# Feed-forward of a decoder trunk: five plain units for six, X put in the PSUM banks by ScalarE, half of the sums of seven products left to TensorE, one tile for the sums of a chunk pair

## The chip, the core and the metric

One core of a Trainium2 chip runs the whole program. The metric is the time of one execution on the device in microseconds (us); lower is better. In the profile PE is TensorE (PEld its weight loads), DVE is VectorE, ACT is ScalarE, POOL is GpSimd, SP is SyncE, which issues nearly all DMAs.

## The reference

A trunk of two layers on 512 tokens of width 1024, all in float32. Each layer is an attention part and a feed-forward part, and a final norm ends it. The attention part is not touched here. The feed-forward part, with 22 chunks of 128 channels in each half of `w_in` (D_FF = 2816):

```python
def conv_glu_ffn(h, w_in, conv_w, conv_b, w_out):
    a, b = jnp.split(h @ w_in, 2, axis=-1)                  # 1024 -> 2 x 2816
    a = causal depthwise convolution of width 3(a) + conv_b
    return (jax.nn.silu(a) * b) @ w_out                      # 2816 -> 1024

x = x + mixer(rmsnorm(x, attn_norm[layer]))
x = x + conv_glu_ffn(rmsnorm(x, ffn_norm[layer]), ...)       # layer 0, then layer 1
```

## The kernel before

**Layout.** Activations lie with channels on the partitions and the 512 tokens along the row. X is eight tiles of 128x512, `X[0]` to `X[7]`. A float32 operand is split in two parts, a rounded one (`h`, an ACT copy with cast) and the rest (`l`, a DVE subtraction), and each product is three matmuls: h by h, l by h, h by l. So every weight tile that is loaded (`wraw`, `wb`, `wo`) costs an ACT cast (`whi`, `sxh`) and a DVE subtraction (`wlo`, `sxl`) before its second matmul can start.

**A plain unit.** Chunk c of `a` or `b` is a unit: eight weight blocks times `XH[k]`, `XL[k]`, 24 matmuls 512 wide, into one PSUM bank (`mm`). Two units make a chunk. DVE multiplies the bank by `rstd` into `a` or `b`; `gate` does the convolution (ACT `tap2`, two DVE `tap`, ACT Silu), `gated` multiplies and splits the result into `gh`, `gl`. The first PLAIN = 6 chunks are done so.

**A seven.** The other 16 chunks are done by `seven(c)`: the 2x2 block product (weights of a and b, two halves of the 1024 channels, two halves of the tokens) with seven products of half the size in place of eight. Each product is 12 matmuls 256 wide. Weight sums `p1` to `p4` are made by `total` and split by `part`; products go to banks `s` (two buffers of two banks), `t` and `o`; seven DVE or ACT operations (`first_a`, `first_b`, `v`, `c12`, `both`, `c11`, `c21`) put the results together. The moving sides of the seven are sums of halves of the normed X, made once per layer by `sums(k)` for the four chunk pairs (k, k+4): two norms on DVE (`gh<-x,ng,rstd`), four 256-wide sums on POOL (`gl<-gh`), four splits. They are made beside the plain units.

**The output.** `out(m, p)` multiplies the gated chunks of part p (PARTS: chunks 0-5, 6-11, 12-16, 17-21) with a block of w_out into a bank `mm`, and DVE adds the bank to `X[m]`. In layer 1 the last part is done token-wise with the final norm (`tokens`).

**Who sets the order.** `Plan` is a list of jobs with engine, cost, dependencies, buffers taken and given, and a priority; `Plan.run` places them one by one and the instructions of every engine are emitted in that order. Engines run them in that order: an instruction that waits holds up all behind it on its engine.

The PE priorities are 100 + chunk for units and products and 200 + part for `out`, so that `out` fills the gaps that products leave:

```python
order[1] = add("PE", 1.45, fn, pj[n], order[1], *TJ, prio=100 + c, take=(take,), give=("slot",))
j = add("PE", 0.685, step, wj, j, GJ[c0 + k], prio=200 + p, ...)
```

All instructions are recorded at line 91 (a wrapper), so the profile's groups are told apart by tile names. `sr` names a weight sum, `sxh`/`sxl` its parts, `b1`, `b2`, `t1`, `t3` (h and l) the moving sums.

Of the kernel before, what the change touches and what calls it, by code (L numbers as in the profile page):

```python
# [18 lines left out]
P = 128  # L19
# [19 lines left out]
PARTS = ((0, 6), (6, 12), (12, 17), (17, 22))  # L39
PLAIN = 6  # L40
# [143 lines left out]
def trunk(ctx, tc, A):  # L184
# [10 lines left out]
    def mm(out, l, r, st, sp_):  # L195
        pe.matmul(out, l, r, start=st, stop=sp_)
# [943 lines left out]
    def ffn(layer, nl, final):  # L1140
# [7 lines left out]
        with ExitStack() as es:  # L1148
            fp = es.enter_context(tc.tile_pool(name=f"fp{layer}", bufs=2))
            first = [weights(A["wfi"][layer, u], [P, NK, P], behind=fed[0] if u else None) for u in range(2)]  # L1150
            plan = Plan(dict(PE=0.0, ACT=2.6, DVE=2.6, POOL=4.9, SP=-5.0), dict(PE=0.03), wraw=2, wb=2, wo=2, w=2, mm=2, s=2, t=1, o=1,
                        a=2, tt=1, b=2, g=10, sr=2, slot=NK, sq=2)
            plan.bufs["w"], plan.bufs["slot"] = [], []
            add = plan.add
            M = Mixer(plan, None, None)
            GH, GL, GJ = {}, {}, {}
            B = {n: [fp.tile([P, H, w], F32R, tag=f"{n}{x}", bufs=1, name=f"{n}{x}") for x in "hl"]
                 for n, w in (("b1", W), ("b2", SEQ), ("t1", SEQ), ("t3", SEQ))}

            MV = dict(b11=("b1", LO), b21=("b2", LO), b22=("b2", HI), t1=("t1", LO), t2=("t1", HI), t3=("t3", LO), t4=("t3", HI))  # L1160
# [4 lines left out]

            def split(h, l, x, n, prio, *deps, take=(), give=()):

                j = add("ACT", 0.19 + 0.00085 * n, lambda: act.copy(h(), x()), *deps, prio=prio, take=take)
                return add("DVE", 0.16 + 0.00104 * n, lambda: dve.tensor_sub(l(), x(), h().bitcast(F32)), j, prio=prio, give=give)
# [54 lines left out]
            def plain(c, root):  # L1224
                box = {}
                ps = []
                for u in range(2):
# [3 lines left out]
                    for k in range(NK):  # L1231
                        def step(k=k, w=w, bx=bx):
                            if k == 0:
                                bx["ps"] = mm_bank()
# [5 lines left out]
                        j = add("PE", 0.685, step, w[1], j, prio=100 + c, take=("mm",) if k == 0 else (), give=give)  # L1240
# [11 lines left out]
                j = add("DVE", 0.69, fa, ps[0][1], root[0], prio=1, take=("a",), give=("mm",))  # L1252
                t = gate(c, box, j)
                j = add("DVE", 0.69, fb, ps[1][1], prio=1, take=("b",), give=("mm",))
# [3 lines left out]
            def sums(k, root):  # L1258

                x = {}  # L1260

                def norm(c):
                    x[c] = g_tile("gh", F32)
                    dve.scalar_tensor_tensor(x[c], X[c], ng[:, nl - 1, c:c + 1], rstd, op0=ALU.mult, op1=ALU.mult)
                    if c >= H:
                        x["d1"], x["d3"] = g_tile("gl", F32), g_tile("gl", F32)
# [8 lines left out]
                part = lambda n, i: (lambda: B[n][i][:, k])  # L1275
                a = split(part("b1", 0), part("b1", 1), lambda: x[k][:, LO], W, p, j, s4)
                b = split(part("b2", 0), part("b2", 1), lambda: x[k + H], SEQ, p, j, s4, give=("g",))
                c = split(part("t1", 0), part("t1", 1), lambda: x["d1"], SEQ, p, s2, s4)
                d = split(part("t3", 0), part("t3", 1), lambda: x["d3"], SEQ, p, s4, c, b, give=("g",))
                TJ.extend((a, b, c, d))  # L1280

            order = [None] * 3
            count = [0]

            def seven(c):

                w, box, sm, sj = [None] * 4, {}, {}, {}
                n0 = c * 0.001

                def load(u, pool_, tag):  # L1290
                    def fn():
                        t = pool_.tile([P, NK, P], F32, tag=tag, bufs=2, name=tag)
# [3 lines left out]
                lb = add("SP", 0.35, load(1, fp, "wb"), M.prev_load, prio=1 + n0, take=("wb",), lat=3.3)  # L1296
                la = M.prev_load = add("SP", 0.35, load(0, wp, "wraw"), lb, prio=1 + n0, take=("wraw",), lat=3.3)

                def total(n, x, y, eng, *deps, give=()):
                    e = (pool, dve)[eng == "DVE"]  # L1300

                    def fn():
                        sm[n] = wp.tile([P, H, P], F32, tag="sq", bufs=2, name="sr")
                        e.tensor_add(sm[n], x(), y())
                    sj[n] = order[2] = add(eng, 1.35 if eng == "POOL" else 0.69, fn, *deps, order[2], prio=1.2 + n0, take=("sr",), give=give)
# [10 lines left out]
                E1, E3 = "DVE", "POOL"  # L1316
                total("p1", lambda: w[2], lambda: w[3], E1, lb)
                part("a1", lambda: w[0], la)
                total("p2", lambda: sm["p1"], lambda: w[0], "DVE", sj["p1"], la)
                part("p2", lambda: sm["p2"], sj["p2"])  # L1320
                part("p1", lambda: sm["p1"], sj["p2"], give=("sr",))
                total("p4", lambda: sm["p2"], lambda: w[1], "DVE", pj["p2"], pj["p1"], give=("sr",))
                part("p4", lambda: sm["p4"], sj["p4"], give=("sr",))
                total("p3", lambda: w[0], lambda: w[2], E3, sj["p4"])
                part("p3", lambda: sm["p3"], sj["p3"], give=("sr",))
# [3 lines left out]
                def product(j, n, m, take):  # L1329
                    t, cols = MV[m]  # L1330

                    def fn():
                        if take == "s":
                            r = box[j] = s_bank()[:, 0:W]
                        else:
                            r = box[j] = bank(names[take], take)[:, 0:W]
                        h, l = parts[n]
                        for k in range(H):
                            xh, xl = B[t][0][:, k, cols], B[t][1][:, k, cols]
                            mm(r, h[:, k], xh, k == 0, False)  # L1340
                            mm(r, l[:, k], xh, False, False)
                            mm(r, h[:, k], xl, False, k == H - 1)
                    order[1] = add("PE", 1.45, fn, pj[n], order[1], *TJ, prio=100 + c, take=(take,), give=("slot",))
# [14 lines left out]

                def both():
                    b = box["b"].rearrange("p (h s) -> p h s", h=2)  # L1360
# [463 lines left out]
```

## Time and profile before

| | |
|---|---|
| time, median of 3 runs (lowest, highest) | 1217.15 us (1217.04, 1217.43) |
| the profiled execution: time, its span | 1217.21 us, 1215.4 us |
| granted TensorE clock | 0.999 |
| busy share PE, DVE, ACT, POOL | 99%, 77%, 53%, 18% |
| layer 0: feed-forward starts; first seven starts | 271.4 us; about 338 us |
| layer 1: feed-forward starts; first seven starts | 855.4 us; about 921 us |
| POOL, all of it | 221.1 us in 262 instructions |

A matmul's row in the timeline lasts from its start to the end of its pipeline, so rows overlap: the pace of TensorE is the distance from one start to the next, and a wait shows as a longer distance. Time "idle before" an instruction is the engine's, with what released it. A row of several instructions ("x2") gives the time from the start of the first to the end of the last.

### The profile page before, as it was taken

The numbers are of one execution on the slowest core, as the hardware profiler recorded it, in microseconds if no ns is written. First come the engines' busy times: TensorE is split into PE (matmuls) and PEld (weight loads), VectorE is DVE, ScalarE is ACT, GpSimd is POOL, SyncE is SP. The second block draws the span as 40 slices with busy tenths as digits, with TensorE's granted clock in tenths as the row PEclk, the third lists the DMA queues.
The fourth block names the chain that finished last, engine by engine and source line by source line (L and its number), as shares of the span: only waits on it lengthen the run. The fifth ranks groups of instructions, "written<-read, shape, count | busy, mean of one in ns | idle before, by whom it ended". The sixth has DMA issues, their size and how long they took to land.

```text
span 1215.4 us, 19513 instructions
## 1 busy us (share of the span) xinstructions
PE 1204.9 (99%) x7476; PEld 1036.9 (85%) x7476; DVE 935.1 (77%) x1603; ACT 643.4 (53%) x1185; POOL 221.1 (18%) x262
## 2 busy tenths in 40 slices
PE   9999999999999999999999999999999999999997
PEld 6887877778898999999887888877888999999996
DVE  6867887579997999888764563456899889988885
ACT  6666577745553454444453664644555445444453
POOL 0000044423310011000121452411341001100000
PEclk9999999999999999999999999999999999999999
DMA  7322231122413231413224452322233233232331
GB/s 236 122 73 92 73 112 36 36 70 87 161 65 122 96 109 62 149 62 126 84 91 150 160 178 83 110 70 87 87 115 129 74 114 127 73 106 79 124 105 70
DMA packets 50685, 124.71 MB, mean 103 GB/s; under 512 B 6096, under 2 KB 16080, under 8 KB 50592
## 3 DMA queue, kind: packets, MB, share of 16 engines
q1 hardware_dynamic: 50304, 123.18, 30.6%
q8 instruction: 59, 0.97, 0.3%
q14 instruction: 34, 0.28, 0.1%
q10 hardware_dynamic: 288, 0.28, 0.1%
HBM read 119.80 MB, written 2.13 MB: 100 GB/s over the span
## 4 chain that ended last, share of the span: by engine, by line
PE 87%; DVE 8%; ACT 2%; issue 2%; POOL 1%; DMA 0%; SPq 0%; DVEq 0%; POOLq 0%; ACTq 0%
PE mm L91 50%; PE s L91 19%; PE t L91 11%; PE o L91 7%; DVE wlo L91 1%; DVE tt L91 1%; POOL e L91 1%; DVE b L91 1%; ACT e L91 1%; DVE sxl L91 1%; DVE gh L91 1%; DVE gl L91 0%; DMA wraw<-wu 0%; DVE a L91 0%; ACT ph L91 0%
## 5 line engine op out<-in xcount | busy, mean ns | idle before, releaser
L91 PE MATMUL mm<-xh,whi 128*128 128x512 f32 x424 | 168.7, 398 | 0.0
L91 PE MATMUL mm<-xh,wlo 128*128 128x512 f32 x424 | 165.5, 390 | 0.0
L91 PE MATMUL mm<-xl,whi 128*128 128x512 f32 x424 | 165.4, 390 | 0.0
L91 DVE TENSOR_TENSOR wlo<-wraw,whi 128x1024 fp32r<-128x1024 f32 (+2 forms) x83 | 100.8, 1214 | 45.0 <-ACT whi L91 44.8
L91 POOL TENSOR_TENSOR sr<-wraw,wb 128x512 f32<-128x512 f32 x32 | 47.4, 1482 | 462.9 <-DVE sr L91 288.1
L91 PE MATMUL mm<-gh,wlo 128*128 128x512 f32 x312 | 122.3, 392 | 0.0
L91 PE MATMUL mm<-gh,whi 128*128 128x512 f32 x312 | 122.2, 392 | 0.0
L91 PE MATMUL mm<-gl,whi 128*128 128x512 f32 x312 | 121.4, 389 | 0.0
L91 ACT CAST sxh<-sr 128x512 fp32r<-128x512 f32 x128 | 76.4, 618 | 83.9 <-DVE sr L91 54.9
L91 ACT CAST whi<-wraw 128x1024 fp32r<-128x1024 f32 (+2 forms) x83 | 81.8, 986 | 65.6 <-PE mm L91 41.8
L91 DVE TENSOR_TENSOR x<-x,mm 128x512 f32<-128x512 f32 x96 | 65.4, 684 | 47.8 <-PE mm L91 47.5
L91 POOL TENSOR_SCALAR e<-e,dn 128x128 f32<-128x128 f32 (+3 forms) x128 | 76.2, 616 | 135.6 <-DVE dn L91 123.2
L91 ACT ACTIVATE tt<-a,conv 128x512 f32<-128x512 f32 x44 | 35.9, 817 | 117.8 <-DVE a L91 117.8
L91 DVE TENSOR_TENSOR sxl<-sr,sxh 128x512 fp32r<-128x512 f32 x128 | 95.2, 761 | 2.7 <-ACT sxh L91 1.9
L91 PEld LDWEIGHTS mm<-xh,whi 128*128 128x128 f32 x424 | 79.6, 188 | 19.2 <-issue 3.7
L91 PEld LDWEIGHTS mm<-xl,whi 128*128 128x128 f32 x424 | 79.6, 188 | 17.2 <-DVE xl L91 0.5
L91 PEld LDWEIGHTS mm<-xh,wlo 128*128 128x128 f32 x424 | 79.7, 188 | 17.0 <-DVE wlo L91 1.6
L91 ACT ACTIVATE e<-e,nm 128x256 f32<-128x256 f32 (+3 forms) x128 | 70.7, 556 | 31.6 <-DVE nm L91 31.4
L91 DVE SCALAR_TENSOR_TENSOR tt<-a,conv,tt 128x510 f32<-128x510 f32 x88 | 72.5, 824 | 8.4 <-ACT tt L91 7.2
L91 PE MATMUL s<-t3l,sxh 128*128 128x256 f32 x256 | 72.4, 283 | 0.0
L91 PE MATMUL s<-t3h,sxl 128*128 128x256 f32 x256 | 72.4, 283 | 0.0
L91 PE MATMUL s<-t3h,sxh 128*128 128x256 f32 x256 | 72.4, 283 | 0.0
(281 smaller groups left out, 3420.8 us busy)
## 6 DMA issues: line engine op xcount, KB each, us to landing
wraw<-wfi SPq DMA_DIRECT2D x56, 512.0 KB
wb<-wfi SPq DMA_DIRECT2D x32, 512.0 KB
wraw<-wu SPq DMA_DIRECT2D x30, 512.0 KB
wo<-wfo SPq DMA_DIRECT2D x32, 384.0 KB
wraw<-wo SPq DMA_DIRECT2D x16, 512.0 KB
wo<-wfo SPq DMA_DIRECT2D x24, 320.0 KB
wraw<-wv SPq DMA_DIRECT2D x10, 512.0 KB
x<-x SPq DMA_DIRECT2D x16, 256.0 KB
```

The lines of the kernel that those rows point to most:

```text
L91: r = f(*a, **k)
```

## The change

1. PLAIN = 5, PARTS = (0-4, 5-10, 11-16, 17-21): one chunk more in each layer is done by `seven` (17 in place of 16). The first two `out` of part 0 are cut in two, so that chunk 4 comes last, and run ahead of the first seven.
2. PE order: units, sevens and outs have one counter (`turn`) as priority, 100 + place, so that a seven's products follow each other and one `out` follows each seven.
3. `out` of the parts 0 to 2 (but for m = 0, 1 of part 0): ACT copies `X[m]` into the bank ahead of the matmuls (`place`), these add onto it, and ACT copies the bank back to `X[m]`. The DVE addition goes.
4. In a seven, product 5 is added by TensorE onto product 0's bank and product 6 onto product 3's (`more`), ACT copies the first sum out (`c11`), `both` and the old `c11` go from DVE. The sum `p3` stays on POOL but needs the loaded weights alone (tile `sp`), and its product comes fourth, that of `p4` fifth. Banks 0 and 3 are the two halves of one tile `s`.
5. `sums(k)`: the two normed chunks and the six sums lie in one tile of 128x2048 (`SX`: `sx`, and for odd k the two `wb` buffers, so the first load into `wb` waits for the last `sums`). POOL makes the sums in three instructions (one 2x256 wide, two 256 wide) in place of four, ACT and DVE split all seven pieces in one instruction each of 128x1792 (`bh`, `bl`). Their priority is 1.2027 and the like (that of the weights of a plain unit is 1.2 + 0.001 per unit); it was 2.0 to 2.3.

```diff
-PARTS = ((0, 6), (6, 12), (12, 17), (17, 22))
-PLAIN = 6
+PARTS = ((0, 5), (5, 11), (11, 17), (17, 22))
+HOLD = 2
+PLAIN = 5
...
             def sums(k, root):
...
-                p = 2 + 0.1 * k
-                j = add("DVE", 0.75, lambda: norm(k), root[0], prio=p, take=("g",))
-                j = add("DVE", 0.75, lambda: norm(k + H), j, prio=p, take=("g",))
-                eng, e, cost = (pool, "POOL", 0.74) if True else (dve, "DVE", 0.42)
-                s1 = add(e, cost, lambda: eng.tensor_sub(x["d1"][:, LO], x[k][:, LO], x[k][:, HI]), j, prio=p)
-                s2 = add(e, cost, lambda: eng.tensor_add(x["d1"][:, HI], x[k + H][:, HI], x["d1"][:, LO]), s1, prio=p)
-                s3 = add(e, cost, lambda: eng.tensor_sub(x["d3"][:, LO], x[k + H][:, HI], x[k][:, HI]), s2, prio=p)
-                s4 = add(e, cost, lambda: eng.tensor_sub(x["d3"][:, HI], x["d1"][:, HI], x[k + H][:, LO]), s3, prio=p)
+                p = 1.2 + 0.0001 * (25,27,65,67)[k]
+                j = add("DVE", 0.75, lambda: norm(k), root[0], prio=p, take=("sx",) if n == 0 else ("wb", "wb"))
+                j = add("DVE", 0.75, lambda: norm(k + H), j, prio=p)
+                j = add("POOL", 1.48, lambda: pool.tensor_sub(two(4, 6), two(1, 3), hi.unsqueeze(1).to_broadcast([P, 2, W])), j, prio=p)
+                j = add("POOL", 1.1, lambda: pool.tensor_add(e1, hi2, d1), j, prio=p)
+                j = add("POOL", 1.1, lambda: pool.tensor_sub(e3, e1, lo2), j, prio=p)
+                j = add("ACT", 0.19 + 0.00085 * NC, lambda: act.copy(BX[0][:, k], x[:, W:]), j, prio=p)
+                TJ.append(add("DVE", 0.16 + 0.00104 * NC, lambda: dve.tensor_sub(BX[1][:, k], x[:, W:], BX[0][:, k].bitcast(F32)), j, prio=p,
+                              give=("sx",) if n == 0 else ("wb", "wb")))
...
-                lb = add("SP", 0.35, load(1, fp, "wb"), M.prev_load, prio=1 + n0, take=("wb",), lat=3.3)
+                lb = add("SP", 0.35, load(1, "wb"), M.prev_load, TJ[-1], prio=1 + n0, take=("wb",), lat=3.3)
...
-                j = product(4, "p3", "t3", "s")
-                c22 = take("DVE", 0.69, both, j, c12, give=("s",))
-                j = product(5, "a2", "b21", "t")
-                c11 = take("DVE", 0.42, lambda: dve.tensor_add(av(LO), av(LO), box[5]), j, u, give=("t",))
+                j = product(3, "p3", "t3", 1)
+                c22 = take("DVE", 0.42, lambda: dve.tensor_sub(bv(HI), av(HI), box[3]), j, v)
+                j = product(4, "p4", "b22", "t")
+                c12 = take("DVE", 0.42, lambda: dve.tensor_sub(av(HI), box[4], av(HI)), j, c22, give=("t",))
+                j = product(5, "a2", "b21", 0, kept, u, more=True)
+                c11 = take("ACT", 0.36, lambda: act.copy(av(LO), box[5]), j)
...
             def out(m, p, use=None, ready=None):
...
+                onto = (use is None or final) and (p > 0 or m > 1)
+                def place():
+                    bx["ps"] = M.bank("mm")
+                    if onto:
+                        act.copy(bx["ps"], X[m])
...
-                j = add("DVE", 0.69, lambda: dve.tensor_add(X[m], X[m], bx["ps"]), j, prio=1, give=("mm",))
+                    if onto:
+                        j = XO[m] = add("ACT", 0.62, lambda: act.copy(X[m], bx["ps"]), fo[0], prio=1, give=(bx["job"],))
```

Two places in the order of instructions. First DVE in the plain stage, from the second norm of the first chunk pair on (both layers alike). `gh<-x` and `wb<-x`, `sx<-x` are norms, `tt` the taps of the chunk before, `wlo<-wraw` the l weights of the fifth unit, without which its second matmul cannot start. Before:

```order
L91 SCALAR_TENSOR_TENSOR gh<-x_1652,ng,rstd 128x512
L91 TENSOR_TENSOR gl<-b,gh 128x512
L91 TENSOR_TENSOR a<-mm,rstd 128x512
L91 SCALAR_TENSOR_TENSOR gh<-x_1646,ng,rstd 128x512
L91 TENSOR_TENSOR wlo<-wraw,whi 128x1024
L91 SCALAR_TENSOR_TENSOR tt<-a,conv,tt 128x510
L91 SCALAR_TENSOR_TENSOR tt<-a,conv,tt 128x511
```

And now, where all lines are one further down:

```order
L92 SCALAR_TENSOR_TENSOR sx<-x_1652,ng,rstd 128x512
L92 TENSOR_TENSOR gl<-b,gh 128x512
L92 TENSOR_TENSOR a<-mm,rstd 128x512
L92 SCALAR_TENSOR_TENSOR wb<-x_1646,ng,rstd 128x2x256
L92 SCALAR_TENSOR_TENSOR wb<-x_1652,ng,rstd 128x512
L92 SCALAR_TENSOR_TENSOR tt<-a,conv,tt 128x510
L92 SCALAR_TENSOR_TENSOR tt<-a,conv,tt 128x511
L92 TENSOR_TENSOR wlo<-wraw,whi 128x1024
L92 TENSOR_TENSOR bl<-sx,bh 128x1792
```

The fifth unit's l weights have moved behind one norm more and both taps.

Second POOL in the feed-forward of layer 1, from the last instruction of the attention part on. Before, the sums of the four chunk pairs are sixteen short instructions, of which these are the first eight:

```order
L91 TENSOR_TENSOR acc<-acc,sq 128x512 x6
L91 TENSOR_TENSOR gl<-gh 128x256
L91 TENSOR_TENSOR gl<-gh,gl 128x256
L91 TENSOR_TENSOR gl<-gh 128x256
L91 TENSOR_TENSOR gl<-gl,gh 128x256
L91 TENSOR_TENSOR gl<-gh 128x256
L91 TENSOR_TENSOR gl<-gh,gl 128x256
L91 TENSOR_TENSOR gl<-gh 128x256
L91 TENSOR_TENSOR gl<-gl,gh 128x256
```

And now all of them, with the 17 weight sums of the sevens behind them:

```order
L92 TENSOR_TENSOR acc<-acc,sq 128x512 x6
L92 TENSOR_TENSOR sx<-sx 128x2x256
L92 TENSOR_TENSOR sx<-sx 128x256 x2
L92 TENSOR_TENSOR wb<-wb 128x2x256
L92 TENSOR_TENSOR wb<-wb 128x256 x2
L92 TENSOR_TENSOR sx<-sx 128x2x256
L92 TENSOR_TENSOR sx<-sx 128x256 x2
L92 TENSOR_TENSOR wb<-wb 128x2x256
L92 TENSOR_TENSOR wb<-wb 128x256 x2
L92 TENSOR_TENSOR sp<-wraw,wb 128x512 x17
```

The first sum of a pair no longer starts after its first norm but, with the others, after the second.

More of the change, by code (lines that the diff above doesn't have):

```diff
@@ L1279, in sums @@
-                d = split(part("t3", 0), part("t3", 1), lambda: x["d3"], SEQ, p, s4, c, b, give=("g",))
-                TJ.extend((a, b, c, d))
+                    out = x[:, SEQ:2 * SEQ] if c >= H else x[:, 0:SEQ].rearrange("p (h w) -> p h w", h=2)[:, ::-1]
+                    src, r = X[c], rstd
+                    if c < H:
+                        src, r = [t.rearrange("p (h w) -> p h w", h=2) for t in (X[c], rstd)]
+                    dve.scalar_tensor_tensor(out, src, ng[:, nl - 1, c:c + 1], r, op0=ALU.mult, op1=ALU.mult)
@@ L1290, in load @@
-                def load(u, pool_, tag):
+                turn[0] += 1
+                at = turn[0]
+                n0 = at * 0.001
+                def load(u, tag):
                     def fn():
-                        t = pool_.tile([P, NK, P], F32, tag=tag, bufs=2, name=tag)
+                        if u:
+                            wide[0] ^= 1
+                            t = WB[:, wide[0]]
+                        else:
+                            t = wp.tile([P, NK, P], F32, tag=tag, bufs=2, name=tag)
@@ L1343, in product @@
-                    order[1] = add("PE", 1.45, fn, pj[n], order[1], *TJ, prio=100 + c, take=(take,), give=("slot",))
+                            xh, xl = BX[0][:, k, cols], BX[1][:, k, cols]
+                            mm(r, h[:, k], xh, k == 0 and not more, False, more)
+                            mm(r, l[:, k], xh, False, False, more)
+                            mm(r, h[:, k], xl, False, k == H - 1, more)
+                    own = ("s",) if j == 0 else (place,) if place in names else ()
@@ L1344, in product @@
+                    order[1] = add("PE", 1.45, fn, pj[n], order[1], *TJ, *deps, prio=100 + at, take=own, give=("slot", *give))
                     return order[1]
@@ L1374, in seven @@
+                c12 = take("DVE", 0.42, lambda: dve.tensor_sub(av(HI), box[4], av(HI)), j, c22, give=("t",))
+                j = product(5, "a2", "b21", 0, kept, u, more=True)
+                c11 = take("ACT", 0.36, lambda: act.copy(av(LO), box[5]), j)
                 t = gate(c, box, c11, c12)
-                j = product(6, "b2", "t4", "s")
-                c21 = take("DVE", 0.42, lambda: dve.tensor_sub(bv(LO), bv(LO), box[6]), j, c22, give=("s",))
+                j = product(6, "b2", "t4", 1, c22, more=True)
@@ L1377, in seven, with out @@
+                c21 = take("DVE", 0.42, lambda: dve.tensor_sub(bv(LO), bv(LO), box[6]), j, give=("s",))
                 gated(c, box, t, c21)
-            fo = [None]
-            def out(m, p, use=None):
+            fo, pl, XO, gone = [None], [None], {}, [None, None]
+            def out(m, p, use=None, ready=None):
                 c0, c1 = PARTS[p]
@@ new lines, in end @@
+                def end():
+                    if onto:
+                        j = XO[m] = add("ACT", 0.62, lambda: act.copy(X[m], bx["ps"]), fo[0], prio=1, give=(bx["job"],))
+                    else:
+                        j = XO[m] = add("DVE", 0.69, lambda: dve.tensor_add(X[m], X[m], bx["ps"]), fo[0], XO.get(m), prio=1, give=(bx["job"],))
+                    gone.append(j)
+                    if use is not None:
+                        use(m, j)
+                steps(range(n - 1))
@@ L1476, in turn @@
                                     pe.transpose(bx["ps"][:, t, i * P:i * P + P], X[4 * h + i][:, (t0 + t) * P:(t0 + t) * P + P], ident)
[L1477 removed]
+                        j = add("PE", 0.9, turn, end, *(xj[m] for m in range(4 * h + 4)), prio=302.5 + 0.1 * h, take=("s",))
                         for t in (t0, t0 + 1):
```

175 lines of the change are left out of this document (88 added, 87 removed).

## The prediction

> **What bounds the kernel now.** I read the busy shares first, then the four stages of the two feed-forward parts by windows (columns: stretch, length, then busy time and count of PE, PEld, DVE, ACT, POOL, then clock, DMA share, GB/s), then two long stretches of the chain that ends last.
>
> ```profile
> PE 1204.9 (99%) x7476; PEld 1036.9 (85%) x7476; DVE 935.1 (77%) x1603; ACT 643.4 (53%) x1185; POOL 221.1 (18%) x262
> ...
> 272.00:337.60 65.60, 65.60 (x287) 53.31 (x286) 61.68 (x81) 37.26 (x55) 21.20 (x17) 1.00 0.34 120
> 337.60:595.00 257.40, 257.14 (x1762) 239.34 (x1762) 224.81 (x369) 119.10 (x201) 23.70 (x16) 1.00 0.29 98
> 856.00:921.40 65.40, 65.40 (x287) 53.36 (x286) 61.10 (x81) 36.94 (x55) 21.76 (x17) 1.00 0.35 120
> 921.40:1177.00 255.60, 255.05 (x1753) 237.56 (x1753) 224.75 (x369) 120.27 (x205) 23.70 (x16) 1.00 0.30 103
> ...
> 277.89 44.00 PE mm L91 x193
> ...
> 523.41 2.88 PE s L91 x24
> ```
>
> TensorE sets the time: it is full in every stage, at a full clock, and paces at 44.00/193 = 0.228 us for a matmul 512 wide and 2.88/24 = 0.120 us for one 256 wide. What counts is PE work and PE waits. The reader is also to see that the plain stage (rows one and three) is the tight one for DVE: 61.1 of 65.4 us, 93%, against 88% among the sevens. A delay on DVE there has little room to be made good.
>
> The waits of PE that the change can touch are few. The first rows are of the list of waits (microseconds, times, longest), the others from the timeline (start, duration; the pace is the distance of starts).
>
> ```profile
> PEld o L91 <- DVE sxl L91: 2.6, 6, 0.6
> ...
> PEld mm L91 <- DVE wlo L91: 1.6, 5, 0.4
> ```
>
> ```profile
> 928.27 0.28 PE L91 MATMUL o<-b2h,sxh 128*128 128x256 f32 x1
> ...
> 928.84 0.39 PE L91 MATMUL o<-b2h,sxl 128*128 128x256 f32 x1 [0.29 <-DVE sxl L91]
> 929.07 0.28 PE L91 MATMUL o<-b2l,sxh 128*128 128x256 f32 x1
> ```
>
> In the fourth product of a seven (bank `o`, weights `p4`) the second matmul starts 0.57 us after the first instead of 0.12, since DVE makes the low half of `p4` too late. It happens in 6 of 32 sevens.
>
> **The change, part by part.** *One chunk more as a seven.* A plain chunk is 48 matmuls of 0.228 us, 10.94; a seven is 84 of 0.120, 10.08. That saves 0.86 us per layer, −1.7 for both. This is plain PE time and is certain.
>
> *The order of products.* `p3`, which POOL makes of loaded weights alone, now comes ahead of `p4`, so `p4` has one product (1.44 us) more; the waits seen above are at most 0.6. I take nearly all of them as gone: −2.4 (bounds 0 and −2.6). The small waits for `wlo` are 1.6 us in the whole program, and I give −0.5, a third, to the changed plain stage and its DVE work (bounds 0 and −1.6).
>
> *X through ScalarE, half of the sums to TensorE.* These are the operations removed from DVE and the nearest rows of the ones that replace them (groups by form: busy, mean ns; then idle before):
>
> ```profile
> L91 DVE TENSOR_TENSOR x<-x,mm 128x512 f32<-128x512 f32 x96 | 65.4, 684 | 47.8 <-PE mm L91 47.5
> ...
> L91 DVE TENSOR_TENSOR b<-b,s 128x512 f32<-128x512 f32 x32 | 21.9, 684 | 4.1 <-PE s L91 2.5
> ...
> L91 ACT COPY a<-s 128x256 f32<-128x256 f32 x32 | 11.9, 373 | 24.0 <-PE s L91 24.0
> ...
> L91 ACT COPY ph<-t 128x512 f32<-128x512 f32 x100 | 53.3, 590 | 19.2 <-PE t L91 19.0
> ...
> L91 ACT CAST sxh<-wraw 128x512 fp32r<-128x512 f32 x64 | 39.4, 615 | 2.2 <-PE mm L91 2.2
> ```
>
> In each layer 22 outs lose a DVE addition of 0.684 (15 us) and gain two ACT copies, one out of a bank (0.590) and one into it. No row here shows a write of ACT into a bank; I take 0.6 from the two ACT rows, bounds half and twice that. So ACT gets about 26 us per layer, of which some 13 us more come with copying the first sum and the seventeenth seven; over the 257 us among the sevens it goes from 119 to about 155, 60%. DVE falls from 225 to about 205, 80%. Neither was the bound there, so this costs and brings nothing in PE time by itself: the room that it makes on DVE is hidden, because only the 2.4 us above were lost to DVE. If that cover went (ACT late with a copy by one 0.6 us) PE would wait for a bank in 44 outs, up to 26 us; I see no reason, with ACT 40% idle and two places of an out between.
>
> *Steady sevens.* Product 5 now opens bank 0 again. In the built program it waits for DVE's `c22`, which reads bank 3 of the same tile. Between product 3 and product 5 stands one product, 1.44 us; `c22` needs the end of product 3 (0.28 us after its last start, by the row at 928.27) and some 0.42 itself, so 0.7 us of slack per seven. It holds if DVE is not held up by an instruction longer than that; I put +0.3 for 34 sevens (bounds 0 and 34 × 0.2 = 6.8).
>
> *The sums in the plain stage: the large term.* They were the last choice of the plan and are now made in the middle of the fifth unit's preparation. DVE and POOL meet there before as well (timeline, layer 1):
>
> ```profile
> 867.76 0.75 POOL L91 TENSOR_TENSOR gl<-gh 128x256 f32<-128x256 f32 x1 [8.90 <-DVE gh L91]
> ...
> 873.38 1.17 POOL L91 TENSOR_TENSOR gl<-gh,gl 128x256 f32<-128x256 f32 x1 [4.87 <-DVE gh L91]
> 874.52 1.30 POOL L91 TENSOR_TENSOR gl<-gh 128x256 f32<-128x256 f32 x1
> 875.78 1.72 POOL L91 TENSOR_TENSOR gl<-gl,gh 128x256 f32<-128x256 f32 x1
> 877.45 1.18 POOL L91 TENSOR_TENSOR gl<-gh 128x256 f32<-128x256 f32 x1
> ```
>
> ```profile
> 868.14 1.70 DVE L91 SCALAR_TENSOR_TENSOR tt<-a,conv,tt 128x510 f32<-128x510 f32 x2
> 869.76 1.22 DVE L91 TENSOR_TENSOR wlo<-wraw,whi 128x1024 fp32r<-128x1024 f32 x1
> ...
> 873.26 0.69 DVE L91 TENSOR_TENSOR gl<-b,gh 128x512 fp32r<-128x512 f32 x1
> 873.87 0.68 DVE L91 TENSOR_TENSOR a<-mm,rstd 128x512 f32<-128x512 f32 x1
> 874.47 0.74 DVE L91 SCALAR_TENSOR_TENSOR gh<-x,ng,rstd 128x512 f32<-128x512 f32 x1
> 875.13 1.76 DVE L91 TENSOR_TENSOR wlo<-wraw,whi 128x1024 fp32r<-128x1024 f32 x1
> 876.82 2.36 DVE L91 SCALAR_TENSOR_TENSOR tt<-a,conv,tt 128x510 f32<-128x510 f32 x2
> ```
>
> ```profile
> 878.31 0.39 PE L91 MATMUL mm<-xh,wlo 128*128 128x512 f32 x1
> ```
>
> Alone `wlo` takes 1.22 and two taps 1.70; beside POOL they take 1.76 and 2.36, and POOL's 0.75 becomes 1.17 to 1.72. (Back to back an instruction takes 0.06 to 0.08 less than its row: norm 0.66, by the starts 874.47 and 875.13, tap 0.80, `wlo` 1.14, a split 0.60.) The rows fit two engines that take turns by whole instructions: POOL 1 ends at 874.55, the norm (0.66) then ends at 875.21, POOL 2 ends 0.6 later at 875.82, `wlo` 1.07 later at 876.89, POOL 3 0.61 later at 877.50. The DVE operation that reads a bank (`a<-mm`) is not lengthened. The Trainium skill has this as a rule ("SBUF — State Buffer", section "Who interferes with whom"): the two engines share a port pair that is an exclusive lock, a DVE operation with two SBUF inputs contends with a POOL operation that reads SBUF, and who blocks is decided by the order of issue; by that rule the delay is what the next paragraph works out, and the trace agrees.
>
> Now the changed order: from the same moment DVE has norm, norm, tap, tap, and only then the `wlo` of the fifth unit, which the row at 878.31 needs. POOL's first instruction is 512 wide; for that size alone there is a row, 1289 ns the fastest of 32:
>
> ```profile
> L91 POOL TENSOR_TENSOR sr<-wraw,wb x32: 1289/1302/1882, 341.3 to 1165.2; 128x512 f32<-128x512 f32 x32
> ```
>
> By turns, on the clock of layer 1: POOL from 873.87 to 875.16, norm to 875.84, POOL (256 wide) to 876.5, norm to 877.17, POOL to 877.84, tap to 878.6, the next pair's first POOL instruction to 879.8, tap to 880.55, POOL to 881.2, `wlo` to 882.4. That is 4.1 us after 878.31, and PE has nothing else to do in its order. Without any hold DVE would need 0.66 + 0.66 + 0.80 + 0.80 + 1.22 from 874.47, to 878.61: 0.3 late. With one turn more it is 4.7. I take 4.1 since these turns fitted the rows above to 0.1 us. Layer 0 has the same order, and its norm at the same place is held as well (0.74 above, 1.33 here):
>
> ```profile
> 290.47 1.33 DVE L91 SCALAR_TENSOR_TENSOR gh<-x,ng,rstd 128x512 f32<-128x512 f32 x1
> ```
>
> So +8.2 for two layers.
>
> *The rest of the plain stage.* Behind that `wlo` DVE has, up to the `wlo` of the second short out, four splits 1792 wide at about 1.95 (an estimate: 0.69 at 512 and 1.22 at 1024, carried on), fifteen instructions 512 wide at 0.60, five more `wlo` at 1.14, six taps at 0.80, four norms at 0.66 and two `wlo` of outs at 0.74: 31.5 us, and 4 to 7 for POOL's turns, 35.5 to 38.5. PE, started 4.1 late, reaches that out 35.3 us after 882.4 (5.2 of the fifth unit, 27.2 of five units, 2.9 of the first short out). Late by 0.2 to 3.2; The two last pairs are six POOL instructions, 2 × (1.29 + 2 × 0.67) = 5.3 us, which would be 1.5 late; some of them fall beside operations that read a bank and hold nobody up, so I take 1.2 per layer, +2.4. The first `wb` load now waits for the last sums; its copy lands in a few us and the first seven is more than 5 us off, so nothing.
>
> *Sum*, from the profiled execution's 1217.2 (0.06 above the median of the runs): −1.7 −2.4 −0.5 +8.2 +2.4 +0.3 = +6.3, **1223.5 us**.
>
> **The rivals.** *A, faster.* POOL does not hold DVE up at this place, because its sums start before or after the two norms (the emitted order fixes each engine's row, not their meeting). Then the fifth unit is 0.3 late per layer and the rest 0.15: 1217.2 − 4.6 + 0.6 + 0.3 + 0.3 = 1213.8. For it speaks that the norm at 874.47 lost only 0.08; against it that `wlo` and the taps lost 1.2 within the same 5 us. It decides when the stalls of both plain stages stay under 1.8 us.
>
> *B, no change.* DVE is slowed in proportion, not blocked: 3.58 us of work took 4.71, a factor of 1.3. The 4.1 us from 874.47 then take 5.4 and end at 879.9, 1.6 late, with POOL busier perhaps 1.9; with 0.3 for the rest that is 1217.2 − 4.6 + 3.8 + 0.6 + 0.3 = 1217.3. Against it: whole turns fit the single rows.
>
> *C, slower still.* The reopened bank stalls TensorE in every seven because `c22` comes late behind a long DVE instruction (a split of 0.8 us is enough to use up the 0.7): 0.2 each on top is 1223.5 + 6.5 = 1230. DVE's 20% of idle time speaks against it.
>
> **How the numbers follow.** Forecast 0.62, C 0.08, B 0.18, A 0.12. A time within 0.2% (2.4 us) is no change for this measurement. So faster 0.12, same 0.18, slower 0.70. The likeliest case alone runs from 1218.9 (3.0 at the fifth unit, nothing behind it) to 1227.5 (4.7, and 2.5 behind it, with a part of the bank's price). The range for 8 in 10 leaves out most of A and C: 1214.8 to 1227.5.
>
> **What would show it.** In the changed kernel's timeline the first `mm<-xh,wlo` of the fifth unit stands some 4 us behind its predecessor with DVE `wlo` as releaser, in both layers, and the norms and taps ahead of it alternate with POOL's `tensor_sub`. No PE wait for `sxl` in the sevens, ACT near 60% and DVE near 80% among them. A few tenths in all before product 5. Wrong it is if the fifth unit starts within 1 us (A, B), or if the list of waits has a row of PE on `s` with DVE `b` of several us (C).

## The result: 1228.07 us, 0.9% slower, and the profile after

| | before | after |
|---|---|---|
| median (lowest, highest) of 6 executions each | 1217.03 us (1216.80, 1217.43) | 1228.07 us (1227.13, 1230.68) |
| ratio | | 1.0093, 95% interval 1.0082 to 1.0105 |
| profiled execution: time, span, mean granted clock | 1217.21, 1215.4, 0.999 | 1227.42, 1225.5, 0.997 |

The direction of the forecast was right; its 1223.5 us is 4.6 short, and the time lies 0.6 us above the range.

The page's first part and four stretches by windows (stretch, length, busy time and count of PE, PEld, DVE, ACT, POOL, granted clock, DMA share, GB/s):

```profile
PE 1205.1 (98%) x7548; PEld 1040.8 (85%) x7548; DVE 903.6 (74%) x1525; ACT 699.1 (57%) x1295; POOL 219.6 (18%) x256
...
272.00:337.60 65.60, 61.13 (x267) 49.50 (x266) 60.67 (x68) 34.36 (x41) 20.55 (x14) 1.00 0.31 110
...
342.00:598.00 256.00, 254.52 (x1778) 238.88 (x1778) 205.55 (x336) 144.20 (x260) 23.71 (x15) 1.00 0.28 99
...
886.00:889.00 3.00, 2.82 (x7) 2.24 (x8) 3.00 (x3) 1.81 (x2) 0.71 (x1) 0.51 0.51 175
889.60:892.00 2.40, 2.40 (x12) 1.93 (x11) 2.40 (x4) 0.62 (x1) 0.00 (x0) 1.00 0.00 0
```

PE is idle for 4.5 us of the plain stage of layer 0, and for 1.5 us among the sevens, where before it was full. DVE's work among the sevens fell from 225 to 206 us (205 forecast) and ACT's rose from 119 to 144 (155 forecast). The fourth row was not foreseen: for 3 us in layer 1 the granted clock is 0.51.

The list of waits, in place of the rows for `sxl` and `wlo` shown of before:

```profile
PEld mm L92 <- DVE wlo L92: 9.7, 6, 3.1
...
PE mm L92 <- DVE wlo L92: 7.5, 4, 2.7
...
PE s L92 <- DVE b L92: 1.8, 4, 0.9
...
PE s L92 <- ACT mm L92: 1.5, 2, 0.7
```

The wait of bank `o` for `sxl` is gone. In its place stand four long waits for `wlo` and six for results of a seven.

The fifth unit in layer 1, in the timeline of DVE, POOL and PE (start, duration):

```profile
878.69 0.68 DVE L92 TENSOR_TENSOR a<-mm,rstd 128x512 f32<-128x512 f32 x1
879.29 2.33 DVE L92 SCALAR_TENSOR_TENSOR wb<-x,ng,rstd 128x512 f32<-128x512 f32 x2
881.55 2.91 DVE L92 SCALAR_TENSOR_TENSOR tt<-a,conv,tt 128x510 f32<-128x510 f32 x2
884.39 1.74 DVE L92 TENSOR_TENSOR wlo<-wraw,whi 128x1024 fp32r<-128x1024 f32 x1
```

```profile
878.20 4.02 POOL L92 TENSOR_TENSOR sx<-sx 128x512 f32<-128x512 f32 x3 [14.31 <-DVE sx L92]
882.18 4.53 POOL L92 TENSOR_TENSOR wb<-wb 128x512 f32<-128x512 f32 x3
```

```profile
883.10 0.39 PE L92 MATMUL mm<-xh,whi 128*128 128x512 f32 x1
886.18 0.79 PE L92 MATMUL mm<-xh,wlo 128*128 128x512 f32 x1 [2.70 <-DVE wlo L92]
886.78 0.63 PE L92 MATMUL mm<-xl,whi 128*128 128x512 f32 x1
...
889.63 0.39 PE L92 MATMUL mm<-xh,whi 128*128 128x512 f32 x1
```

The second matmul starts 3.08 us after the first instead of 0.23: 2.86 us, as much in layer 0. The two norms and two taps have 2.33 and 2.91 us while POOL works. Behind the stall the matmuls follow each other at 0.43 us instead of 0.23 until 889.6, which costs 1.6 us and is the stretch at half the clock.

The second short output of layer 0 waits 1.93 us for its `wlo`, which runs beside POOL's first `p3`:

```profile
332.55 1.90 DVE L92 TENSOR_TENSOR wlo<-wo,whi 128x640 fp32r<-128x640 f32 x1
```

```profile
332.27 1.48 POOL L92 TENSOR_TENSOR sp<-wraw,wb 128x512 f32<-128x512 f32 x1 [10.09 <-DMA wraw<-wfi]
```

In layer 1 `p3` comes 0.6 us behind this `wlo`, which takes 0.82, and the output waits 0.50.

A stall ahead of product 5, the second seven of layer 0:

```profile
359.06 0.28 PE L92 MATMUL t<-bl,sxh 128*128 128x256 f32 x1
359.88 0.36 PE L92 MATMUL s<-bh,sxh 128*128 128x256 f32 x1 [0.54 <-DVE b L92]
```

```profile
356.41 1.45 DVE L92 TENSOR_TENSOR sxl<-wraw,sxh 128x512 fp32r<-128x512 f32 x1
357.79 0.68 DVE L92 TENSOR_TENSOR sxl<-wb,sxh 128x512 fp32r<-128x512 f32 x1
358.39 0.41 DVE L92 TENSOR_TENSOR a<-b,o 128x256 f32<-128x256 f32 x1
358.72 0.68 DVE L92 TENSOR_TENSOR sxl<-wraw,sxh 128x512 fp32r<-128x512 f32 x1
359.32 0.41 DVE L92 TENSOR_TENSOR b<-a,s 128x256 f32<-128x256 f32 x1
```

```profile
352.49 4.82 POOL L92 TENSOR_TENSOR sp<-wraw,wb 128x512 f32<-128x512 f32 x1 [12.88 <-DVE sxl L92]
```

Product 5 would start at 359.18. It waits until `c22` (`b<-a,s`) ends at 359.73, since `c22` reads bank 3 of its tile. `c22` is last in a row of DVE instructions without a gap, one of which took 1.45 us instead of 0.68 when POOL's `p3` got its turn. By distances of starts such stalls are 0.70, 0.90 and 0.35 us in layer 0 and 1.01, 0.90 and 0.36 in layer 1, 4.2 us, with 0.5 in the matmuls behind.

### The profile page after: what moved, and what is told of

It is laid out like the page before. It is cut to its first block, busy times and chain, and to the rows that moved or that the text cites. A ratio compares the mean times of both kernels' runs of the same rounds, so it can differ in the third digit from the quotient of the medians.

```text
span 1225.5 us, 19687 instructions
## 1 busy us (share of the span) xinstructions
PE 1205.1 (98%) x7548; PEld 1040.8 (85%) x7548; DVE 903.6 (74%) x1525; ACT 699.1 (57%) x1295; POOL 219.6 (18%) x256
## 4 chain that ended last, share of the span: by engine, by line
PE 80%; DVE 11%; ACT 4%; issue 2%; POOL 1%; DMA 1%; SPq 0%; DVEq 0%; ACTq 0%; POOLq 0%
PE mm L92 44%; PE s L92 19%; PE t L92 10%; PE o L92 7%; DVE wlo L92 2%; DVE b L92 2%; DVE tt L92 2%; POOL wb L92 1%; DVE sxl L92 1%; DVE gl L92 1%; DVE sr L92 1%; DVE wb L92 1%; ACT whi L92 1%; DVE bl L92 1%; DMA wb<-wfi 1%
## 5 line engine op out<-in xcount | busy, mean ns | idle before, releaser
L92 PE MATMUL s<-bh,sxh 128*128 128x256 f32 x544 | 154.3, 284 | 3.3 <-DVE b L92 1.8
L92 PE MATMUL mm<-xh,whi 128*128 128x512 f32 x392 | 156.7, 400 | 0.0
L92 PE MATMUL s<-bl,sxh 128*128 128x256 f32 x544 | 153.9, 283 | 0.0
L92 PE MATMUL s<-bh,sxl 128*128 128x256 f32 x544 | 153.9, 283 | 0.0
L92 PE MATMUL mm<-xl,whi 128*128 128x512 f32 x392 | 153.7, 392 | 0.0
L92 POOL TENSOR_TENSOR sp<-wraw,wb 128x512 f32<-128x512 f32 x34 | 50.1, 1475 | 414.7 <-DVE sxl L92 315.6
L92 PEld LDWEIGHTS s<-bh,sxh 128*128 128x128 f32 x544 | 104.2, 192 | 5.7 <-ACT mm L92 1.8
L92 PEld LDWEIGHTS s<-bh,sxl 128*128 128x128 f32 x544 | 104.3, 192 | 1.3
L92 PEld LDWEIGHTS s<-bl,sxh 128*128 128x128 f32 x544 | 104.3, 192 | 0.0
L92 ACT CAST sxh<-sr 128x512 fp32r<-128x512 f32 x102 | 61.5, 621 | 65.1 <-DVE sr L92 59.8
```

The costliest lines, as they stand in the source:

```text
L92: r = f(*a, **k)
```

## The experiments

The theory after these views: (1) POOL's and DVE's turns make the fifth unit and the short outputs late, and the place of the fifth unit's weights in DVE's row makes it worse; (2) the shared tile makes product 5 wait for `c22`, which a backlog of DVE makes late. The rivals: DVE's own work fills the plain stage; DVE is short of time among the sevens whatever the tile.

The kernel before ran beside each at 1217.0 to 1217.3 us. In kernels on the changed one's plan the plan is made as before, and only its finished row of jobs is edited, so nothing else moves.

### Two tiles for a seven's two banks

```diff
-                        if j == 0:
-                            box["s"] = s_banks()
+                        if j in (0, 3):
+                            box["s", place] = s_banks()
...
-                            r = box[j] = box["s"][:, place, 0:W]
+                            r = box[j] = box["s", place][:, 0, 0:W]
```

> The changed kernel with the two banks that a seven fills twice (products 0 and 5, products 3 and 6) in two tiles instead of the two halves of one; the order on every engine is the same. If product 5 is held only because the tile is shared (it waits for DVE's reader of product 3 in the other bank), the six stalls ahead of product 5 (4.2 us in both layers) and 0.5 us beside them go: 1228.1 - 4.5 = 1223.6. If DVE is simply short of time there, the stall moves to product 6 or to the next weight part, and the time stays within 1 us of 1228.

The edit takes both buffers of `s` for one seven and uses one bank of each; the order on every engine stays.

Measured: 1224.57 us, ratio 1.0059 (1.0046 to 1.0072). All six stalls are gone. But `c22` itself is no longer late. The same seven with two tiles (DVE, PE):

```profile
360.42 0.42 DVE L92 TENSOR_TENSOR b<-a,s 128x256 f32<-128x256 f32 x1
...
361.66 0.28 PE L92 MATMUL s<-bh,sxh 128*128 128x256 f32 x1
```

It ends 0.8 us before product 5 begins; in the changed kernel it ended 0.55 after that product was due. The row of ACT that copies the first sum out (`c11`) tells why, first in the changed kernel, where product 5 begins at 359.88, then with two tiles:

```profile
363.07 0.37 ACT L92 COPY a<-s 128x256 f32<-128x256 f32 x1 [1.56 <-PE s L92]
```

```profile
363.35 0.37 ACT L92 COPY a<-s 128x256 f32<-128x256 f32 x1 [0.73 <-PE s L92]
```

3.19 us after the start of product 5 in one tile, 1.69 with two; in all 34 sevens it is 3.1 to 3.4 against 1.6 to 2.0. That is 0.1 us behind the end of the last matmul of product 6 in the one and of product 5 in the other. The gate of the chunk follows `c11`. This is the first tap of the gate that belongs to the seven before, in DVE's row, again first in the changed kernel:

```profile
350.07 0.75 DVE L92 SCALAR_TENSOR_TENSOR tt<-a,conv,tt 128x510 f32<-128x510 f32 x1 [1.97 <-ACT tt L92]
```

```profile
351.11 0.75 DVE L92 SCALAR_TENSOR_TENSOR tt<-a,conv,tt 128x510 f32<-128x510 f32 x1 [0.53 <-ACT tt L92]
```

DVE waits 1.97 us for ACT in place of 0.53, starts this tap 9.11 us ahead of the time at which product 5 is due in place of 10.55, and has no gap from there to `c22`. So the tile makes two false waits: ACT's `c11` waits one product, 1.44 us, too long, in every seven; the gate and DVE's work on it come so much later, into the next seven; there `c22` is late, and product 5 waits for it.

### The fifth unit's weights first

The edit takes this unit's `wlo` job out of the finished row and puts it back ahead of the first norm into `wb`:

```diff
+                o.remove(w)
+                o.insert(o.index(n), w)
```

> The changed kernel with one DVE instruction per layer moved: the l weights of the fifth unit ahead of the two norms of the second chunk pair. If the place of this instruction is the cause, the two stalls of 2.86 us go, and with them the lower clock after the second one (1.6 us): 1228.1 - 7.3 = 1220.8. If DVE is the bound of the plain stage, what is saved there comes back at the second short output (1.9 and 0.5 us now): 1224 to 1228.

Measured: 1231.54 us, ratio 1.0110 (1.0094 to 1.0125): not faster. My theory of the place fell; the wait came back, as the rival said, but the time lies above the rival's range as well. The one execution of four with a granted clock of 0.998 took 1228.11 us, the three with 0.996 took 1231.5 to 1231.7, so what is above the range goes with the lower clock.

```profile
290.34 1.72 DVE L92 TENSOR_TENSOR wlo<-wraw,whi 128x1024 fp32r<-128x1024 f32 x1
...
300.51 1.22 DVE L92 TENSOR_TENSOR wlo<-wraw,whi 128x1024 fp32r<-128x1024 f32 x1
```

```profile
301.79 0.50 PE L92 MATMUL mm<-xh,wlo 128*128 128x512 f32 x1 [1.37 <-DVE wlo L92]
```

The fifth unit has its weights 2 us early; the sixth waits 0.3 us at its start and 1.6 at its second matmul, a later unit 0.7, the second short output 2.3, in both layers, and the clock dips twice. DVE with POOL's turns is full there in either order.

### POOL's sums without reading

```diff
-lambda: pool.tensor_sub(two(4, 6), two(1, 3), hi.unsqueeze(1).to_broadcast([P, 2, W]))
+lambda: pool.memset(two(4, 6), 0.5)
```

and the other two sums likewise.

> The changed kernel, but POOL fills the sums of the plain stage with a constant and reads nothing (the sums are left out of the computation); the order is the same. If DVE is late because the two engines hold each other up for whole instructions when both read SBUF, the norms and taps go back to 0.66 and 0.80 us each, the fifth unit is at most 0.4 us late, the second short output not at all: 1228.1 - 5.1 - 1.6 - 2.4 = 1219, and less if the first sevens' stalls are this backlog (down to 1215). If DVE is late by the order of its instructions alone: 1226 to 1228.

Measured: 1218.60 us, ratio 1.0012 (1.0004 to 1.0021). The same DVE rows in layer 0, and a place in layer 1 where POOL's fills lie beside a `wlo`:

```profile
289.87 1.41 DVE L92 SCALAR_TENSOR_TENSOR wb<-x,ng,rstd 128x512 f32<-128x512 f32 x2
291.19 1.53 DVE L92 SCALAR_TENSOR_TENSOR tt<-a,conv,tt 128x510 f32<-128x510 f32 x2
292.64 1.22 DVE L92 TENSOR_TENSOR wlo<-wraw,whi 128x1024 fp32r<-128x1024 f32 x1
```

```profile
885.97 1.04 POOL L92 MEMSET wb<- 128x512 f32 x3 [4.10 <-DVE bl L92]
...
886.37 1.22 DVE L92 TENSOR_TENSOR wlo<-wraw,whi 128x1024 fp32r<-128x1024 f32 x1
```

In the same row of instructions, norms, taps and `wlo` fall by 0.92, 1.38 and 0.52 us, 2.8 together, the stall itself. Fifth unit, short outputs (0.2 left) and clock are clean: 9.5 us, the price of POOL's reading sums. The fills of the first two pairs read no norm and ran ahead of them (859.37 and 860.34 in layer 1), so at the fifth unit POOL is not there at all; that a POOL that only writes does not lengthen the `wlo` beside it (1.22) is shown by the one place above. The six stalls ahead of product 5 stay (0.36 to 1.02), so they are not a backlog of the plain stage.

### POOL's p3 without reading

```diff
-                    pool.tensor_add(sm["p3"], w[0], w[2])
+                    pool.memset(sm["p3"], 0.5)
```

> The changed kernel, but POOL fills the weight sum p3 of every seven with a constant and reads nothing (that sum is left out of the computation). If POOL's p3 makes DVE late in the sevens, the stalls ahead of product 5 go: about 1224. If the first sevens suffer from the backlog of the plain stage or the shared tile alone, they stay at 359.9 and 374.3 us: 1226 to 1228.

Measured: 1224.79 us, ratio 1.0062 (1.0050 to 1.0075). Four of the six stalls are gone, the two of 0.36 stay; the clock dipped in both layers. `c11` is as late as before (3.1 to 3.2 us after product 5's start in the sevens that stalled), but where product 5 stalled most `c22` now ends 0.22 and 0.35 us before it is due. POOL's turns with `p3` are thus a part of what makes `c22` late, beside the late `c11`.

### Sums on DVE, two tiles

```diff
-lambda: pool.tensor_sub(two(4, 6), two(1, 3), hi.unsqueeze(1).to_broadcast([P, 2, W]))
+lambda: dve.tensor_sub(two(4, 6), two(1, 3), hi.unsqueeze(1).to_broadcast([P, 2, W]))
```

and the other two likewise, at the same places of the row.

> The kernel with two tiles (1224.6 us), and the sums of the plain stage made by DVE at the places where POOL's stood in the plan: per chunk pair 0.60 + 2 x 0.33 = 1.3 us of DVE's own work in place of waits for POOL's 2.6 us. If POOL's turns are what DVE is late by, the fifth unit is still about 2 us late (1.9 us of sums now stand ahead of its weights), but the second short output is no longer: 1224.6 - 1.6 - 3.4 - about 1 of lower clock = 1218.6. If DVE's own work is the bound, sums on DVE change nothing: 1223 to 1226.

Measured: 1219.02 us, ratio 1.0015 (1.0006 to 1.0023). The stalls left by distances of starts: 1.89 at the fifth unit of each layer, 1.51 at layer 0's short output. The same sums, 1.3 us of DVE's own work per pair, cost less than POOL's turns.

### X by DVE again

```diff
-                    if onto:
-                        act.copy(bx["ps"], X[m])
...
-lambda: act.copy(X[m], bx["ps"])
+lambda: dve.tensor_add(X[m], X[m], bx["ps"])
```

> The kernel with two tiles and the sums on DVE, with one part undone: X is again added to the outputs' banks by DVE (44 additions of 0.68 us back on DVE, 88 ACT copies gone; the order is the same). If this relief of DVE is hidden among the sevens, as forecast, the time is that of the kernel with two tiles and the sums on DVE within 1 us. If DVE needs the room, its weight parts come late again: 2 to 6 us more.

Measured: 1218.92 us, ratio 1.0013 (1.0004 to 1.0022), as with the sums on DVE alone. The sevens of layer 0 with X by ACT and with X by DVE, by windows:

```profile
337.60:595.00 257.40, 257.40 (x1805) 242.16 (x1804) 210.23 (x340) 148.57 (x267) 20.91 (x16) 1.00 0.29 100
```

```profile
337.60:595.00 257.40, 257.40 (x1806) 242.15 (x1805) 222.55 (x362) 128.41 (x224) 21.73 (x16) 1.00 0.29 100
```

12 us of DVE's work and 20 of ACT's change places, and PE is full in both: this part is hidden.

### Before with five plain units alone

```diff
-PLAIN = 6
+PLAIN = 5
```

> The kernel before with one part of the change alone: five plain units in place of six, the sums' orders and all else by its own plan. By the PE work alone 1217.1 - 1.7 = 1215.4. If the sums, late in the plan and on POOL, no longer fit into the shorter plain stage, PE waits ahead of the first seven: 1218 to 1225.

Measured: 1242.58 us, ratio 1.0208 (1.0194 to 1.0222), far above both.

```profile
335.50 0.79 PE L91 MATMUL mm<-gh,whi 128*128 128x512 f32 x1 [8.31 <-ACT whi L91]
```

The sums, last in the old plan, do not fit into the shorter stage: the first output waits 8.5 us for ACT, which has them ahead of it. With the old plan's late sums five plain units cost 25 us; whether earlier sums alone would mend that was not tried on this kernel.

### One piece per unit

`n`, `q` and `f` are norms, sums and splits of a chunk pair; `u` counts the plain units.

```diff
+                for u, js in ((3, n[0][1:] + q[0] + n[1][:1]), (4, f[0]), (5, n[1][1:] + q[1]), (6, f[1]), (7, n[2] + q[2][:1]),
+                              (8, q[2][1:] + f[2]), (9, n[3] + q[3][:1]), (10, q[3][1:] + f[3])):
...
+                    i = o.index(at_unit[u]) + 1
+                    o[i:i] = js
```

> The kernel with two tiles and the sums on DVE, and besides the norms, sums and splits of the four chunk pairs dealt out one piece per plain unit, each behind the l weights of a unit. If the plain stage has room for this work on DVE (18 us beside 3.1 of 5.4 us per unit) and only its place was wrong, no unit waits: before's 1217.1 - 1.7 for one chunk more as a seven - 2.3 for p4 - 0.3, about 1213. If DVE has not the room, the stall stands at a later unit or at the short outputs: 1217 to 1221.

Measured: 1236.52 us, ratio 1.0160 (1.0146 to 1.0173). In this row the first load into `wb` stands ahead of the last sums, which so use other data. The list of waits:

```profile
PE mm L92 <- ACT whi L92: 10.5, 4, 5.2
```

ACT's last split (`bh`) now stands ahead of the output's `whi` and waits for sums on DVE, which themselves wait 1.99 us for that load. A row dealt out by hand moved the stall; it says nothing of the room.

### Another row, then p3 on DVE

For these rows the plan's jobs were run through in their engines' order with the durations of the last kernel's trace, and DVE's jobs exchanged while the end became earlier; the kernel then takes the row as a list:

```diff
+                return o[:34] + [o[i] for i in ROW] + o[34 + len(ROW):]
```

> The kernel with two tiles and the sums on DVE (1219.0 us), with another row of the same DVE instructions around the fifth unit: a norm goes into the 0.9 us in which DVE waits for ACT, and the fifth unit's l weights come ahead of the second tap and of one sum. The row was worked out from the durations of that kernel's trace; in it the 1.89 us ahead of the fifth unit are gone and no later unit waits. If so, 1219.0 - 3.8 = 1215.2 or, with fewer dips of the clock, down to 1213.5: faster than before's 1217.1. If the plain stage is full on DVE, the wait comes back at the sixth unit or at the short outputs: 1217 to 1219.

Measured: 1218.48 us, ratio 1.0008 (0.9999 to 1.0016). The fifth unit is in time, but the sixth waits 0.96 us, and the short outputs 1.91 and 0.66. As the rival said.

```diff
-                    pool.tensor_add(sm["p3"], w[0], w[2])
+                    dve.tensor_add(sm["p3"], w[0], w[2])
```

> The kernel with the other row, and besides the weight sum p3 of every seven on DVE in place of POOL (34 instructions more of 0.60 us on DVE, no more turns with POOL in the feed-forward). If the remaining 1.5 us ahead of the second short output in layer 0 are a turn with POOL's first p3, they shrink to 0.9 or less, and nothing else changes as the sevens have room: 0 to 1.5 us faster than the kernel with the other row. If DVE has no room among the sevens: 2 us slower or more.

Measured: 1216.69 us, ratio 0.9995 (0.9986 to 1.0004). Layer 0's short output waits 0.54 instead of 1.91, and its `wlo` takes 0.82 instead of 1.89 beside POOL's first `p3`: it was a turn with that. Layer 1's, where `p3` had not met it, waits 0.90 instead of 0.66.

### A second row: faster than both

```diff
-                return o[:34] + [o[i] for i in ROW] + o[34 + len(ROW):]
+                return o[:40] + [o[i] for i in ROW] + o[40 + len(ROW):]
```

> The kernel with p3 on DVE (1216.7 us) with a second row of the same DVE instructions over the whole plain stage, worked out from that kernel's durations (taps 0.73 each, an ACT result 0.17 us later, the load of the activation table 1.28 us); by these the waits that it still has in both layers (0.96 + 0.95 at the sixth unit with 0.3 beside them, 0.54 + 0.90 at the short output) are gone. If so: 1216.7 - 3.6 = 1213.1, faster than before. If the room is not there: no change, 1216 to 1217.

Measured: 1212.37 us, ratio to before 0.9960 (0.9947 to 0.9974). The page, and layer 0 by windows:

```profile
PE 1200.8 (99%) x7548; PEld 1039.6 (86%) x7548; DVE 897.8 (74%) x1583; ACT 701.0 (58%) x1295; POOL 133.2 (11%) x198
...
272.00:337.60 65.60, 65.60 (x304) 54.52 (x303) 61.64 (x85) 37.07 (x48) 1.30 (x1) 1.00 0.33 114
337.60:595.00 257.40, 257.40 (x1793) 241.66 (x1792) 208.01 (x357) 148.19 (x265) 0.00 (x0) 1.00 0.30 100
```

PE is full in both stages; the waits over 0.1 us in the feed-forwards are those at their first unit (0.4), which before has too. DVE has 61.6 of 65.6 us: the room is there, just.

### The second row with one tile

The first diff of this section, undone.

> The kernel with the second row, with the two banks of a seven in one tile again, as in the changed kernel. If the stalls ahead of product 5 need DVE to be behind (by POOL's turns or by the plain stage), which it is not here, the time is that of the second row within 1 us; the wait of 0.36 us at the fourth or fifth seven of each layer may stay (0.7). If the shared tile alone makes them: 3 to 4.5 us slower.

Measured: 1219.71 us, ratio 1.0020 (1.0012 to 1.0029): 7.3 us more than with two tiles, and more than the 3 to 4.5 of the rival. My theory, that DVE must be behind by POOL or by the plain stage, fell.

```profile
PE s L92 <- DVE b L92: 5.6, 6, 1.3
...
354.53 0.28 PE L92 MATMUL t<-bl,sxh 128*128 128x256 f32 x1
356.14 0.35 PE L92 MATMUL s<-bh,sxh 128*128 128x256 f32 x1 [1.33 <-DVE b L92]
```

The plain stage is clean and POOL idle, and three sevens of each layer stall all the same, for 1.49, 0.82 and 0.96 us, with 0.2 in the matmuls behind them. ACT waits for banks `s` in all 34 sevens again, where with two tiles (second row) it does in 22:

```profile
ACT a L92 <- PE s L92: 80.2, 34, 7.0
```

```profile
ACT a L92 <- PE s L92: 37.1, 22, 6.3
```

So the tile makes these stalls without POOL's turns and without a late plain stage. The part of the late `c11` can be read from `c22` in the same three sevens: with two tiles it ends 0.43 us after product 5 is due, 0.36 before and 0.54 before; with one tile 1.34, 0.67 and 0.90 after. In the first of them `c22` would thus be late even without it. DVE's load counts too: `p3` is 0.60 us of DVE's own work here, and where it cost DVE nothing ("POOL's p3 without reading") two of the three sevens were in time with one tile. All that stall are among the first six sevens of a layer, which with two tiles follow each other at 13.5 us, later ones at 14.2 and more; whether that is why was not tried.

## Why the prediction was right and wrong

| term | forecast | measured | from |
|---|---|---|---|
| chunk as a seven, `p4`, small waits | −4.6 | −4.8 | second row against before, with all new waits gone |
| fifth unit | +8.2 | +5.7 | 2 × 2.86 |
| rest of the plain stage | +2.4 | +2.4 | short outputs, 1.93 + 0.50 |
| reopened bank | +0.3 | +4.7 | six stalls 4.2, 0.5 behind them |
| lower clock | not foreseen | +1.6 | eight matmuls at 0.43 us, layer 1 |

The measured terms make 9.6 of the 10.2 us between the two profiled executions; 0.6 is not accounted for. Part of the forecast's nearness is errors that cancel: the fifth unit was 2.5 us too high, the bank 4.4 and the clock 1.6 too low. The agreement of the third row is luck: 1.2 was forecast for each layer, and layer 0's 1.93 contains 1.08 of a turn with POOL's first `p3` (1.90 for a `wlo` of 0.82), which the forecast did not have.

**The step that failed** is the one on steady sevens. It named the false wait of product 5 for `c22` and bounded it by 34 × 0.2 = 6.8, but took 0.3, from 0.7 us of slack and DVE's mean load. It did not look for other waits that the same tile makes: `c11` on ACT, 1.44 us too late in every seven, takes that slack and more where DVE has no gap. I had looked at the waits of PE alone. The slack itself was about right: in most of the sevens that do not stall `c22` ends 0.7 to 0.8 us before product 5 is due. So rival C's place came true beside the forecast, in 6 sevens of 34 at 0.8 us each, and the long DVE instruction that it named was only a part of the cause: ahead of the four longer stalls a DVE instruction of 0.68 us took 1.45 to 1.79 by a turn with `p3`, on top of the late `c11`; ahead of the two of 0.36 none did. A second term was put at nothing: the lower clock, 1.6 us, behind the stall that was forecast.

**The fifth unit** was the forecast's mechanism, and the rule held: the engines take turns by whole instructions, and without POOL's reading sums the loss is gone. It is not as strict everywhere: the `p3` at 352.49 above took 4.82 us and stood behind six DVE instructions without a bank among their operands, up to 356.08, where DVE reads one; why it got no turn earlier stays open. At the fifth unit the turns came in the very order of the forecast: POOL 512 wide, norm, POOL, norm, POOL, tap, POOL 512 wide, tap, POOL, `wlo`. The size was 1.2 us per layer too large, because every step was shorter. From the end of one engine's instruction to the end of the other's in the trace it is 0.54 to 0.55 us for a norm or a tap (0.67 to 0.76 in the forecast), 0.6 for POOL 256 wide (0.65 to 0.67), 1.15 for 512 wide (1.2) and 1.08 for `wlo` (1.2), together 1.0 us of the 1.2. The tap had been misread: the pair at 868.14 that counted as alone, 1.70 us, overlaps POOL's row at 867.76; two taps without POOL take 1.53. The Trainium skill ("SBUF — State Buffer", section "Who interferes with whom") says that a POOL instruction that only writes does not contend with a DVE instruction's second input; the trace agrees, with a `wlo` of 1.22 us beside POOL's fills.

**Rivals A and B.** B's price, 3.8 for the fifth units, is not far from 5.7; the total does not tell it from whole turns, the rows do: no one factor fits them (1.4 for `wlo`, 1.6 for the norms and the first tap, 2.2 for the second tap, which stands behind POOL's 512-wide instruction). A fell.

**The hidden parts** were right: X by ACT is worth nothing, as tried with two tiles and the sums on DVE. The range was too narrow because it took in "a part of the bank's price" and no drop of the clock.

## What to carry to other kernels

When work is put back onto a bank, look at everyone who reads or writes the tile that holds it, on all engines: two banks in one tile are one for the waits, and here that cost 3.5 and 7.3 us where two tiles cost nothing. Work given to an idle engine that takes turns with the busy one can cost the busy one more than doing it itself (1.3 us of DVE's own per chunk pair, where POOL's turns at one pair lengthened DVE's norms, taps and `wlo` by 2.8). In a stage that is nearly full, one instruction moved forward only moves the wait; the row has to be made as a whole, from measured durations.

## What was not expected of the hardware

After a PE stall of 2.3 to 2.9 us TensorE may run at half its clock for about 3 us: granted clock 0.51, matmuls 512 wide at 0.43 us. It came after the 2.86 us in layer 1 of the changed kernel and not after the same 2.86 us in layer 0; with two tiles it was the other way round; after 1.93 us or less it was never seen here.

The traces settle which stall does it. Every stretch at half the clock inside a program lasts 3.41 us or two or three times that, and the stretches of one execution begin a whole number of 3.41 us apart (335.86 and 926.36 us in the run with the fifth unit's weights first: 173 times 3.413). So the clock is set window by window. The four windows around the two stalls of the changed kernel, layer 0's stall across two of them, layer 1's in one, and the one behind that:

```profile
292.12:295.53 3.41, 2.22 (x10) 1.50 (x8) 3.37 (x4) 1.80 (x2) 3.33 (x3) 1.00 0.00 0
295.53:298.94 3.41, 1.90 (x8) 1.59 (x9) 3.41 (x2) 2.78 (x3) 1.97 (x2) 1.00 0.27 83
...
882.62:886.03 3.41, 0.86 (x4) 0.38 (x2) 3.37 (x3) 2.81 (x3) 3.25 (x3) 1.00 0.00 0
886.04:889.45 3.41, 3.27 (x8) 2.59 (x9) 3.31 (x4) 1.77 (x2) 0.67 (x1) 0.50 0.45 154
```

PE is idle for 1.2 and 1.5 us of the first two and the clock stays; it is idle for 2.6 of the third and the next window has half the clock. In all traces of this case the ten full-clock windows in which PE was idle for 1.99 us or more were followed by half the clock, and none with 1.95 or less was (idle by the profile's busy time, whose matmul ends are modelled). The windows lie otherwise in each execution, so whether a stall of 2 to 3 us costs some 1.6 us more is chance.

With that goes the spread of the changed kernel's executions, 3.6 us, with granted clocks of 0.998 in the fastest and 0.994 in the slowest; the second row's spread over 0.9. The Trainium skill ("TensorE: Matmul & The Clock Gate", section "What's actually happening") gives an idle window of about 3.4 us, free-running, before the clock is halved; the length and the free run agree with these traces, but here windows that were idle for 2.0 of their 3.41 us did it.
